# State decay and decayed scan products of the second head group moved from VectorE to ScalarE, and the chunk norm's Newton step done column by column

## The chip, the cores and the metric

The kernel runs on one core of one Trainium2 chip. Its time is device microseconds (us) of one execution of the program, and a result is the median over several executions. The core has five engines that run their own instruction queues and meet by semaphores: TensorE (PE in the profile, with PEld for its weight loads), VectorE (DVE), ScalarE (ACT), GpSimd (POOL) and SyncE (SP), which here issues all transfers.

## The reference

One layer of a hybrid generator over 1024 latent tokens of width 1024, with a prefix of 256 context tokens. A token mixer takes the normalised and modulated tokens through one input projection, whose columns feed three heads: a bidirectional state-space scan (8 heads of width 64 in two groups of four, state size 128, chunks of 128 tokens), a Fourier mix of width 256, and a pooling mix of width 256. They are joined by one output projection; then come a normalisation, and a gated feed-forward net of width 2816 with a 3x3 convolution. What the change touches is this part of the scan:

```
decay_states = jnp.exp(A_cs[..., -1:] - A_cs)
states = jnp.einsum("bclhn,bhcl,bclhp->bchpn", B, decay_states, X)
...
y_off = jnp.einsum("bclhn,bchpn,bhcl->bclhp", C, states, jnp.exp(A_cs))
return (y_diag + y_off).reshape(b, L, h, p), final_state
...
y = (y * jax.nn.silu(z.astype(jnp.float32))).reshape(bsz, L, SSD_GROUPS, SSD_WIDTH // SSD_GROUPS)
y = (y * lax.rsqrt(jnp.mean(y * y, -1, keepdims=True) + EPS)).reshape(bsz, L, SSD_WIDTH)
```

The state of each direction is multiplied at every chunk by one number per head and increased by the chunk's own contribution. The output of a chunk has a part from the state that came in, multiplied by one number per token, head and direction. The gated output is normalised over each group of 256 columns.

## The kernel before

All tensors are float32. Where TensorE needs accuracy, an operand is split into a rounded high part and a low part (`split`, lines 216 to 219: ACT writes the high part, POOL or DVE the difference), and three products are added. The program runs its stages in a row: input projection and context (0 to about 240 us), the scan, Fourier and pooling heads (to about 390), the output projection `pout` (line 1010), first normalisation (`post1`), and the feed-forward net from about 495 us to the end.

The scan has three pieces of code that matter here.

- `state_step` (lines 704 to 717), 7 steps for each of two directions: POOL weights a chunk's inputs (`xw`, line 685), TensorE makes the contribution `pst` (line 710) in PSUM, DVE multiplies the old state by `etot` (line 712, 128 tokens' worth of state rows by 512 columns: 2 groups x 4 heads x 64) and adds `pst` (line 715), and SP stores the state to DRAM (line 717). Steps 0 to 6 are spread over the projections `pf` and `pp` that feed the Fourier and the pooling head.
- `chunk_y` (line 894), once for each of 8 chunks in the order 4, 5, 6, 7, 3, 2, 1, 0: POOL starts `y` (line 900), TensorE makes `po` for either group (line 908, in PSUM, 2 directions x 4 heads x 64 columns) and `pd` (line 912), DVE multiplies both `po` tiles by the decays `ecs` into `t1` (line 914, one instruction of 512 columns per group), adds `pd` (line 918) and both directions of `t1` (line 920, twice), and multiplies by the gate (line 921). ACT takes squares with sums (line 924) and a logarithm and an exponential for a first inverse root `r` (lines 927, 928).
- `chunk_norm` (line 931) makes `r` better by one Newton step for both groups at once (`newton` with n = 2, lines 146 to 150: four instructions on a tile of 2 columns) and multiplies `y` by it (line 935). `chunk_out` (line 937) transposes `y` on TensorE (`pyt`, line 940), and ACT writes it with its weights (line 944).

`Y(i)` (line 947) writes the norm of the last chunk, the products of this one, and the output of the last one, in this order. The eight of them stand between the projections, the Fourier transforms (`four_chan` line 784, `four_dft` line 802), the pooling (`pool_sums`, `pool_res`, lines 834 to 864) and the preparation of the output weights (`wo_prep`, line 967: multiply by the gate row `g1b`, line 975, and split). The order in which the text issues instructions is not the order on the engines: a scheduler beneath the kernel places each engine's instructions by its own costs, within the dependencies and the buffers. So a change of one instruction also moves others.

PSUM holds two large tiles and four small ones (`psb`); `po`, `pd`, `pst` and `pyt` are all small ones, so TensorE's next product waits until an earlier tile has been read.

## Time and profile before

| | |
|---|---|
| time, median of 3 executions | 1211.18 us (1209.03 to 1214.26) |
| the profiled execution | 1215.51 us |
| its span, first to last instruction | 1213.7 us |
| busy: PE, PEld, DVE, ACT, POOL | 1130.9, 918.5, 991.2, 459.9, 590.2 us |
| mean granted TensorE clock | 0.981 |

The page gives busy time, idle time and the releaser of the idle time for groups of instructions. A tile's name comes without its number (`t<-po,ecs` is `t1` made from `po` and `ecs`). In rows of the timeline the first number is the start in us, the second the length in us of the row's instructions from the first's start to the last's end, and the bracket at the end is the idle time of the engine just before, with what ended it. "x4" stands for four instructions in a row. Where two instructions follow without a pause, the second starts a little before the first's end, so the time that one more instruction costs an engine is the distance of starts.

### The profile page before, as it was taken

The numbers are of one execution on the slowest core, as the hardware profiler recorded it, in microseconds if no ns is written. First come the engines' busy times: TensorE is split into PE (matmuls) and PEld (weight loads), VectorE is DVE, ScalarE is ACT, GpSimd is POOL, SyncE is SP. The second block draws the span as 40 slices with busy tenths as digits, with TensorE's granted clock in tenths as the row PEclk, the third lists the DMA queues.
The fourth block names the chain that finished last, engine by engine and source line by source line (L and its number), as shares of the span: only waits on it lengthen the run. The fifth ranks groups of instructions, "written<-read, shape, count | busy, mean of one in ns | idle before, by whom it ended". The sixth has DMA issues, their size and how long they took to land.

```text
span 1213.7 us, 15187 instructions
## 1 busy us (share of the span) xinstructions
PE 1130.9 (93%) x5328; PEld 918.5 (76%) x5328; DVE 991.2 (82%) x1407; ACT 459.9 (38%) x790; POOL 590.2 (49%) x470
## 2 busy tenths in 40 slices
PE   4899998889878998999999989999999999999986
PEld 2698887768756887788777768888888888888864
DVE  4788787688899889798999956877887787878866
ACT  2263566621444133342231333333333434333553
POOL 0010122244254024573465386767676767676756
PEclk9999999999989999999999999999999999999988
DMA  9849475557525314214545445555555565555513
GB/s 314 282 154 321 139 202 169 158 195 234 183 78 192 119 48 163 89 58 141 167 157 160 125 151 185 181 186 187 191 191 186 178 191 191 191 187 187 186 48 139
DMA packets 151875, 206.48 MB, mean 170 GB/s; under 512 B 12253, under 2 KB 89067, under 8 KB 151799
## 3 DMA queue, kind: packets, MB, share of 16 engines
q1 hardware_dynamic: 151799, 205.51, 52.4%
q8 instruction: 42, 0.69, 0.2%
q14 instruction: 34, 0.28, 0.1%
HBM read 148.76 MB, written 56.71 MB: 169 GB/s over the span
## 4 chain that ended last, share of the span: by engine, by line
PE 58%; DVE 17%; DMA 11%; POOL 4%; ACT 4%; issue 4%; SPq 1%; DVEq 0%; POOLq 0%; ACTq 0%
PE pu L1349 20%; PE pdn L1187 13%; PE pu L1521 6%; PE pout L1010 4%; DMA bc<-cs_scratch 3%; PE pl L1576 3%; PE pz L344 2%; PE p L1349 2%; PE px L445 2%; DVE cv L1234 2%; PE pu L1245 1%; DMA wa<-in_w_ada_dram 1%; DMA ctxr<-in_ctx_dram 1%; DMA wdr<-in_ffn_w_down_dram 1%; ACT EU L645 1%
## 5 line engine op out<-in xcount | busy, mean ns | idle before, releaser
L1234 DVE SCALAR_TENSOR_TENSOR cv<-pu,ffc,cv 128x945 f32<-128x945 f32 (+6 forms) x362 | 425.6, 1180 | 74.6 <-ACT cv L1212 64.9
L1187 PE MATMUL pdn<-wd,gh 128*128 128x512 f32 x576 | 182.2, 397 | 6.6 <-DVE xt L1190 6.1
L1187 PEld LDWEIGHTS pdn<-wd,gh 128*128 128x128 f32 x576 | 108.4, 189 | 33.4 <-DVE xt L1190 7.8
L1190 DVE TENSOR_TENSOR xt<-xt,pdn 128x512 f32<-128x512 f32 x128 | 87.3, 682 | 33.3 <-PE pdn L1187 28.2
L1187 PE MATMUL pdn<-wd,gl 128*128 128x512 f32 x288 | 114.1, 396 | 0.0
L219 POOL TENSOR_TENSOR wul<-wur,wuh 128x1024 fp32r<-128x1024 f32 x29 | 71.6, 2469 | 57.3 <-ACT wuh L218 42.4
L1449 POOL TENSOR_TENSOR wdr<-wdr,g2b 128x512 f32<-128x512 f32 x44 | 57.4, 1308 | 61.5 <-DMA wdr<-in_ffn_w_down_dram 61.5
L219 POOL TENSOR_TENSOR S<-wur,S 128x384 fp32r<-128x384 f32 (+2 forms) x75 | 62.1, 854 | 31.3 <-ACT S L218 30.6
L1212 ACT ACTIVATE cv<-pu,ffc 128x1024 f32<-128x1024 f32 (+3 forms) x46 | 53.5, 1165 | 43.8 <-PE pu L1349 22.1
L1475 POOL TENSOR_TENSOR cv<-cv,cv 128x512 f32<-128x512 f32 x44 | 58.6, 1351 | 22.2 <-ACT cv L1474 22.2
L1349 PE MATMUL pu<-T,S 128*128 128x512 f32 x270 | 67.1, 392 | 0.0
L644 POOL TENSOR_TENSOR bc<-bc,ncs 128x256 f32<-128x256 f32 x32 | 25.8, 810 | 79.4 <-DMA bc<-cs_scratch 68.7
L1187 PEld LDWEIGHTS pdn<-wd,gl 128*128 128x128 f32 x288 | 54.4, 189 | 12.9
L1349 PE MATMUL pu<-h2h,wuh 128*128 128x512 f32 x150 | 59.9, 400 | 3.4 <-ACT pu L1370 3.4
L219 POOL TENSOR_TENSOR gl<-cv,gh 128x512 fp32r<-128x512 f32 x44 | 57.2, 1320 | 10.9 <-ACT gh L218 10.0
L1474 ACT ACTIVATE cv<-cv 128x512 f32<-128x512 f32 x44 | 25.5, 626 | 91.8 <-DVE cv L1234 91.8
L1349 PEld LDWEIGHTS pu<-T,S 128*128 128x128 f32 x270 | 50.7, 188 | 11.6
L1349 PE MATMUL pu<-h2h,wul 128*128 128x512 f32 x150 | 59.5, 396 | 0.0
L1349 PE MATMUL pu<-h2l,wuh 128*128 128x512 f32 x150 | 59.2, 395 | 0.0
L206 POOL TENSOR_TENSOR h2l<-h2t,h2h 128x512 fp32r<-128x512 f32 x14 | 20.6, 1478 | 77.6 <-DVE h2h L205 77.6
L219 POOL TENSOR_TENSOR wd<-wdr,wd 128x512 fp32r<-128x512 f32 x42 | 53.7, 1301 | 4.4 <-ACT wd L218 4.2
L1521 PE MATMUL pu<-h2h,wuh 128*128 128x512 f32 x176 | 55.6, 397 | 0.0
(407 smaller groups left out, 2923.5 us busy)
## 6 DMA issues: line engine op xcount, KB each, us to landing
xt<-x_scratch SPq DMA_DIRECT2D x144, 256.0 KB
x_scratch<-xt SPq DMA_DIRECT2D x144, 256.0 KB
wur<-in_ffn_w_up_dram SPq DMA_DIRECT2D x44, 512.0 KB
wad<-in_w_ada_dram SPq DMA_DIRECT2D x32, 512.0 KB
wdr<-in_ffn_w_down_dram SPq DMA_DIRECT2D x44, 256.0 KB
wa<-in_w_ada_dram SPq DMA_DIRECT2D x32, 256.0 KB
bc<-cs_scratch SPq DMA_DIRECT2D x32, 256.0 KB
xr<-in_x_dram SPq DMA_DIRECT2D x8, 512.0 KB
```

Of the source, the lines that this page charges most:

```text
L219: return (eng or G).tensor_tensor(lo, raw, hi.bitcast(F32), op=ALU.subtract)
L644: G.tensor_tensor(bc[:, 1], bc[:, 1], ncs[:, ch, b : b + 2].unsqueeze(2).broadcast_to([P, 2, P]), op=ALU.add)
L1010: TE.matmul(pt[:, nb * 512 : nb * 512 + 512], u, v[:, nb * 512 : nb * 512 + 512], start=first and i == 0, stop=last and i == 2)
L1187: TE.matmul(pt, u_, wd[nb][:, v_, :], start=i == 0, stop=i == n - 1)
L1190: V.tensor_tensor(xt, xt, pt, op=ALU.add)
L1212: tap[0] = S.activation(acc[:, a * 64 : b * 64], pt[:, a * 64 : b * 64], AF.Identity, bias=ffc[:, 396 + ct : 397 + ct], scale=factor(0, 0))
L1234: last = V.scalar_tensor_tensor(dst, pv[:, r0 + dy : r1 + dy, c0 + dx : c1 + dx], factor(dy, dx), dst, op0=ALU.mult, op1=ALU.add)
L1349: TE.matmul(dst, a[k][u], b[k][w], start=start and k == 0 and j == 0, stop=k == n - 1 and j == 2, skip_group_check=True)
L1449: G.tensor_tensor(raw, raw, g2b[:, s], op=ALU.mult)
L1475: G.tensor_tensor(acc[:, s], acc[:, s], acc_v[:, s], op=ALU.mult)
L1521: TE.matmul(pt[:, q * 512 : q * 512 + 512], a[:, k, :], b[q][:, k, :], start=k == 0 and j == 0, stop=k == KD - 1 and j == 2)
L1576: TE.matmul(accs[t][nb], u_, wd[nb][:, v_, :], start=t < NHALF and m == 0 and i == 0, stop=m == NG - 1 and i == 2, skip_group_check=t >= N ...
```

## The change

Three edits. (1) In `state_step`, DVE multiplies only the first group of the state (256 columns); ACT multiplies the second in four instructions of 64 columns, one per head, with the decay as a scale that is one number per partition. (2) In `chunk_y`, DVE makes the product of the first group only; ACT makes the second group's in eight instructions of 64 columns. (3) `chunk_norm` runs `newton` with n = 1 for each of the two groups (lines 141 to 144: three instructions on one column, in which `r` and `v` are also the per-partition scalars) and multiplies each half of `y` by its own column.

```diff
         dst, src = qt(stag[d](), f"st{d}_{n + 1}", [P, 2, 256]), state[d]
-        V.tensor_tensor(dst[:].rearrange("p g (h q) -> p g h q", q=64),
-                                      src[:].rearrange("p g (h q) -> p g h q", q=64),
-                                      dv(etot, ch, d).unsqueeze(3).broadcast_to([P, 2, 4, 64]), op=ALU.mult)
+        V.tensor_tensor(dst[:, 0].rearrange("p (h q) -> p h q", q=64), src[:, 0].rearrange("p (h q) -> p h q", q=64),
+                        dv(etot, ch, d)[:, 0].unsqueeze(2).broadcast_to([P, 4, 64]), op=ALU.mult)
+        for h in range(4):
+            S.activation(dst[:, 1, h * 64 : h * 64 + 64], src[:, 1, h * 64 : h * 64 + 64], AF.Identity,
+                         scale=etot[:, ch, 8 + 4 * d + h : 9 + 4 * d + h])
         V.tensor_tensor(dst, dst, pt[:].rearrange("p (g n) -> p g n", g=2), op=ALU.add)
...
-        for g in range(2):
-            V.tensor_tensor(t1[:, g].rearrange("p d (h q) -> p (d h) q", q=64),
-                            pos[g][:].rearrange("p (a q) -> p a q", q=64),
-                            ecs[:, ch, g * 8 : g * 8 + 8].unsqueeze(2).broadcast_to([P, 8, 64]), op=ALU.mult)
+        V.tensor_tensor(t1[:, 0].rearrange("p d (h q) -> p (d h) q", q=64), pos[0][:].rearrange("p (a q) -> p a q", q=64),
+                        ecs[:, ch, 0:8].unsqueeze(2).broadcast_to([P, 8, 64]), op=ALU.mult)
+        for a in range(8):
+            S.activation(t1[:, 1, a // 4, (a % 4) * 64 : (a % 4) * 64 + 64], pos[1][:, a * 64 : a * 64 + 64], AF.Identity,
+                         scale=ecs[:, ch, 8 + a : 9 + a])
...
         V.tensor_scalar(v, ssq, 1.0 / 256.0, EPS, op0=ALU.mult, op1=ALU.add)
-        r = newton(r, v, 2, f"ssn{ch}")
-        V.tensor_tensor(yv, yv, r.unsqueeze(2).broadcast_to([P, 2, 256]), op=ALU.mult)
+        for g in range(2):
+            q = newton(r[:, g : g + 1], v[:, g : g + 1], 1, f"ssn{ch}{g}")
+            V.tensor_scalar(yv[:, g], yv[:, g], q, None, op0=ALU.mult)
```

The added lines shift what follows: line 715 before is 717 now, 918 is 921, 920 is 923, 921 is 924, 933 is 936, 935 is 939, 940 is 944, 971 is 975 and 975 is 979. The order on the engines changes between about 243 and 400 us of the old span; behind that it is the same but for a few transfers. Three places are spoken of below.

TensorE, where the projection `pp` of the second half of the pooling columns meets the first chunk's transposes (`pyt`, of chunk 4) and the Fourier head's products (`pft`, `pex`). Before, and then now:

```order
L445 MATMUL pp_2891<-hl_193,wp_h 128x512
L445 MATMUL pp_2891<-hl_194,wp_h 128x512
L940 MATMUL pyt_2837<-ident,y_2762 128x128 x4
L784 MATMUL pft_2870<-PQW,f_2469 128x128 x4
L784 MATMUL pft_2876<-PQW,f_2469 128x128 x4
L787 MATMUL pex_2882<-fex_2478,PQW 128x2
L908 MATMUL po_2928<-S_2794,cT_1341 128x256 x2
```

```order
L445 MATMUL pp_2966<-hh_191,wp_h 128x512
L445 MATMUL pp_2966<-hh_192,wp_h 128x512
L944 MATMUL pyt_2912<-ident,y_2818 128x128 x2
L786 MATMUL pft_2945<-PQW,f_2477 128x128 x4
L786 MATMUL pft_2951<-PQW,f_2477 128x128
L944 MATMUL pyt_2912<-ident,y_2818 128x128 x2
L786 MATMUL pft_2951<-PQW,f_2477 128x128 x3
L789 MATMUL pex_2957<-fex_2486,PQW 128x2
L445 MATMUL pp_2966<-hl_193,wp_h 128x512
```

Between the last `pd` of chunk 5 and the transposes of chunk 4 stood 23 pairs of `pp` matmuls; now 10 stand there, and 13 follow.

VectorE, at the first two chunks (`y_2762` and `y_2818` are chunk 4's `y`, `y_2807` and `y_2875` chunk 5's; `wor` is an output weight that waits for `g1b`). Before, directly behind the multiplication of `wor`, and then now:

```order
L914 TENSOR_TENSOR t_4_2764<-po_2765,ecs 128x512
L914 TENSOR_TENSOR t_4_2764<-po_2768,ecs 128x512
L918 TENSOR_TENSOR y_2762<-y_2762,pd_2771 128x512
L920 TENSOR_TENSOR y_2762<-y_2762,t_4_2764 128x512 x2
L918 TENSOR_TENSOR y_2807<-y_2807,pd_2816 128x512
L921 TENSOR_TENSOR y_2762<-y_2762,z_2655 128x512
```

```order
L915 TENSOR_TENSOR t_4_2820<-po_2821,ecs 128x512
L979 TENSOR_TENSOR wor_3176<-wor_3176,g1b 128x1024
L921 TENSOR_TENSOR y_2818<-y_2818,pd_2827 128x512
L923 TENSOR_TENSOR y_2818<-y_2818,t_4_2820 128x512 x2
L924 TENSOR_TENSOR y_2818<-y_2818,z_2695 128x512
```

The weight's multiplication went from ahead of the first product to behind it.

SyncE, at the last states (`st_6`, `st_7`) and the load of `g1b`. Before, and then now:

```order
L717 DMA s_scratch<-st_6_2716 128x512
L971 DMA g1b<-ada_scratch 128x1024
L717 DMA s_scratch<-st_7_2737 128x512
L717 DMA s_scratch<-st_7_2746 128x512
L886 DMA S_2794<-s_scratch 128x1024
```

```order
L719 DMA s_scratch<-st_6_2760 128x512
L719 DMA s_scratch<-st_7_2785 128x512
L975 DMA g1b<-ada_scratch 128x1024
L719 DMA s_scratch<-st_7_2798 128x512
L888 DMA S_2857<-s_scratch 128x1024
```

The load of `g1b` went behind the store of the first of the last two states.

## The prediction, made before the changed kernel was run

> **What bounds the kernel now.** I read the busy time by stretch first. Each row gives the stretch, its length, then busy us (and instructions) of PE, PEld, DVE, ACT and POOL, the granted clock, and DMA.
>
> ```profile
> 240.00:290.00 50.00, 44.90 (x202) 36.76 (x201) 42.19 (x82) 8.58 (x17) 23.63 (x23) 0.97 0.63 209
> 290.00:390.00 100.00, 82.76 (x415) 67.92 (x415) 93.11 (x145) 39.42 (x101) 40.94 (x20) 0.93 0.50 158
> 390.00:440.00 50.00, 50.00 (x218) 39.94 (x217) 37.76 (x97) 10.26 (x23) 0.00 (x0) 1.00 0.31 110
> 440.00:495.00 55.00, 50.48 (x244) 40.87 (x243) 52.13 (x113) 22.75 (x44) 27.05 (x16) 0.97 0.34 111
> 495.00:1160.00 665.00, 654.00 (x2808) 528.56 (x2807) 552.89 (x544) 233.78 (x367) 435.24 (x351) 0.99 0.52 167
> ```
>
> The reader is to see that the change sits in the first two rows, and that they differ. From 240 to 290 us PE is busy for 44.9 of 50, so work taken from DVE there lies mostly behind matmuls. From 290 to 390 DVE is busy for 93.1 of 100 and PE for only 82.8: here DVE sets the pace and PE loses 17.2 us. From 390 on PE runs without a gap, and what follows moves as a whole when PE gets there earlier. So the change is worth what it takes from PE's 17.2 us, plus a little ahead of them. The largest of PE's waits, from its timeline:
>
> ```profile
> 291.82 1.13 PE L908 MATMUL po<-S,cT 128*128 128x256 f32 x4 [0.40 <-DVE t L914]
> ...
> 307.75 0.93 PE L940 MATMUL pyt<-ident,y 128*128 128x128 f32 x4 [2.34 <-DVE s L863]
> ...
> 343.68 0.73 PE L1010 MATMUL pout<-woh,yh 128*128 128x512 f32 x2 [1.87 <-ACT yh L218]
> ...
> 360.11 1.98 PE L871 MATMUL ppool<-pT,PQW 128*128 128x512 f32 x4 [2.55 <-DVE pT L864]
> ...
> 386.65 1.08 PE L940 MATMUL pyt<-ident,y 128*128 128x128 f32 x4 [3.03 <-DVE y L935]
> ```
>
> Four of the five end with DVE: each time PE has caught up with DVE's queue. The last, at 386.65, is chunk 1's transpose; behind it PE is never short again. So DVE's progress up to the end of chunk 1's norm counts.
>
> **The change part by part.** First the scan products (edit 2) and the price of one DVE instruction:
>
> ```profile
> L914 DVE TENSOR_TENSOR t<-po,ecs 128x512 f32<-128x512 f32 x16 | 10.5, 681 | 0.8 <-PE po L908 0.7
> ...
> 296.00 1.28 DVE L914 TENSOR_TENSOR t<-po,ecs 128x512 f32<-128x512 f32 x2
> ...
> 284.60 1.28 DVE L712 TENSOR_TENSOR st<-st,etot 128x512 f32<-128x512 f32 x2
> ...
> L811 DVE TENSOR_TENSOR f<-py,yo 128x256 f32<-128x256 f32 x2 | 0.8, 412 | 0.0
> ```
>
> Of 16 products of 0.68 us, 8 leave DVE. Two in a row take 1.28, so one costs the queue 1.28 - 0.68 = 0.60 us. Seven of the eight lie ahead of the wait at 386.65 (chunk 0's comes behind it): 7 x 0.60 = **-4.2 us** on DVE's path. PE's wait of 0.40 at 291.82 is for a small PSUM tile that DVE frees late, behind its load of `g1b`; now the first group's tile is freed ahead of that and the second's by ACT: **-0.4**.
>
> What ACT takes over has no row of its size. The nearest are these; the last two show how long PE's own `pd` takes and when the next stage of PE began:
>
> ```profile
> L944 ACT ACTIVATE yT<-pyt,col 128x128 f32<-128x128 f32 x32 | 9.3, 367 | 22.2 <-PE pyt L940 22.2
> ...
> 308.72 1.15 ACT L944 ACTIVATE yT<-pyt,col 128x128 f32<-128x128 f32 x4 [5.23 <-PE pyt L940]
> ...
> L158 ACT ACTIVATE pn_s<-pn_v 128x1 f32<-128x1 f32 x16 | 3.2, 203 | 26.4 <-DVE pn_v L156 26.4
> ...
> 313.59 1.89 PE L912 MATMUL pd<-xt,M 128*128 128x64 f32 x16
> ...
> 319.05 1.89 PE L908 MATMUL po<-S,cT 128*128 128x256 f32 x8
> ```
>
> With 128 columns one more costs (1.15 - 0.37) / 3 = 0.26 us; a single column lasts 0.20. For 64 columns I take 0.23 (bounds 0.15 and 0.26). Eight are 8 x 0.23 + 0.13 = 2.0 us, starting when `po` is complete. In that time PE is at `pd` for 1.9 us, and DVE cannot add `pd` (0.68) before; the additions of `t1` come after that, at about 2.5 us. So the eight lie behind `pd`, if ACT is free. It is busy for 39.4 of 100 us and gets 64 x 0.23 = 14.7 more. I take 0; if another ACT instruction of 1 us is ahead each time, the chunk is late by 0.5, and over seven chunks that is at most +3.5.
>
> **The state decay (edit 1).** Half of 14 multiplications leaves: 14 x (0.68 - 0.41) = 3.8 us of DVE, between 243 and 287 us. What hides it is `pf` and `pp` on PE. Only PE's idle time can give something, and its largest piece is this one, with the two transfers that matter at the end of the stretch and who waits for the second:
>
> ```profile
> 265.13 1.08 PE L738 MATMUL pPQ<-cf 128*128 128x64 f32 x8 [3.40 <-DMA cf<-in_fnet_w_dram]
> ...
> 261.25 0.32 SPq L717 DMA_DIRECT2D s_scratch<-st  x1
> ...
> 285.07 0.44 SPq L971 DMA_DIRECT2D g1b<-ada_scratch  x1
> ...
> 286.50 1.03 SPq L717 DMA_DIRECT2D s_scratch<-st  x2
> ...
> 289.94 1.22 DVE L975 TENSOR_TENSOR wor<-wor,g1b 128x1024 f32<-128x1024 f32 x1 [2.87 <-DMA g1b<-ada_scratch]
> ```
>
> The second part of `cf` was queued behind the store of a state at 261.25, and now stands ahead of both stores; it can be issued about 0.7 us earlier: **-0.7** (0 to -1.5). Against it stands the wait that this edit adds: the addition of `pst` now waits for ACT's four pieces. Where two steps follow each other, as at 284.60, DVE needed 4 x 0.60 = 2.4 us; now the second direction's pieces end at 8 x 0.23 + 0.13 = 2.0 and its addition takes 0.68, so 2.7, that is 0.3 late. Behind these additions are queued the stores, and behind the first store now also `g1b`: it was issued at 285.07 and would go at about 286.0 to 286.8. It took 289.94 - 285.07 = 4.9 us to arrive, so DVE's multiplication of `wor`, and behind it in DVE's queue chunk 4's additions, start at 291 to 291.7 in place of 289.94. But one product stands ahead of it now (0.60) and one is gone (0.60), so chunk 4's last addition is at most 0.6 late, or as it was. I take 0 and keep +1.5. If the cover of PE's matmuls were gone in steps 0 to 5, each step would cost some 0.3, in all +2.
>
> **The norm (edit 3).** The old chain where nothing disturbs it, two Newton chains on one column interleaved (from `post1`), and a multiplication of 1024 columns by scalars:
>
> ```profile
> 360.16 0.16 DVE L146 TENSOR_TENSOR ssn_t<-sr 128x2 f32<-128x2 f32 x1
> ...
> 361.56 1.22 DVE L975 TENSOR_TENSOR wor<-wor,g1b 128x1024 f32<-128x1024 f32 x1
> ...
> 466.73 0.27 DVE L141 TENSOR_SCALAR ln_t<-ln_r,ln_v 128x1 f32<-128x1 f32 x1
> ...
> 467.54 0.20 DVE L175 TENSOR_SCALAR ln_nmr<-ln_mv,ln_q 128x1 f32<-128x1 f32 x1
> ...
> 473.22 0.80 DVE L320 TENSOR_SCALAR xn<-xa,ln_mv,ln_q 128x1024 f32<-128x1024 f32 x1
> ...
> 473.94 1.28 DVE L170 BATCH_NORM_STATS2 pn_st<-xa 128x6 f32<-128x512 f32 x2
> ```
>
> Old: from 360.16 to 361.56, 1.40 us for four small instructions and the multiplication. New: six small ones took 467.54 - 466.73 = 0.81. The multiplication of 1024 columns costs 473.94 - 473.22 = 0.72; a [128,1] instruction about 0.13; so 256 columns cost 0.13 + 0.59 / 4 = 0.28, and two 0.56. New: 1.37. I take 0, with 0.2 either way for seven chunks: -1.5 to +1.5.
>
> The small instructions also meet POOL:
>
> ```profile
> 303.35 2.39 POOL L975 TENSOR_TENSOR wor<-wor,g1b 128x1024 f32<-128x1024 f32 x1 [9.96 <-DVE s L843]
> ...
> 303.37 2.38 DVE L150 TENSOR_TENSOR ssn_q<-sr,ssn_t 128x2 f32<-128x2 f32 x1
> ...
> 446.89 5.08 POOL L206 TENSOR_TENSOR h2l<-h2t,h2h 128x512 fp32r<-128x512 f32 x3 [1.50 <-DVE h2h L205]
> ...
> 447.25 0.27 DVE L141 TENSOR_SCALAR pn_t<-pn_r,pn_v 128x1 f32<-128x1 f32 x1
> ...
> L914 DVE TENSOR_TENSOR t<-po,ecs x16: 672/680/693, 291.1 to 387.0; 128x512 f32<-128x512 f32 x16
> ...
> L920 DVE TENSOR_TENSOR y<-y,t x16: 676/692/2661, 293.0 to 390.1; 128x512 f32<-128x512 f32 x16
> ```
>
> An old Newton instruction of two columns was held for all of POOL's 2.39 us; the one-column form ran in its usual 0.27 under POOL. So the new chain is not held. But the next instruction, the multiplication of `y`, reads SBUF like those that are held, so the stall goes to it: 0, bounds -2 to 0. The last two rows speak against edit 2: the product from PSUM never lasts longer than 0.69, while the addition from SBUF to SBUF goes up to 2.66. The Trainium skill has a rule for this ("SBUF — State Buffer", section "SBUF: two separate sides"): VectorE and GpSimd share a port pair as an exclusive lock, which a VectorE instruction needs if it has two SBUF inputs, and one from PSUM does not. The trace agrees with it in these rows. By it the edit takes away the very work that DVE could do while POOL holds the port; what that makes of the time is the second rival.
>
> **The sum.** -4.2 - 0.4 - 0.7 = **-5.3 us**, so 1215.51 - 5.3 = 1210.2 for an execution like the profiled one. That one was 4.3 us above the median of the runs shown; against the median it is 1211.18 - 5.3 = **1205.9 us**, 0.44% less. The unknown terms (ACT late +3.5, `g1b` +1.5, norm -1.5 to +1.5, stall -2, `cf` -0.8 to +0.7) seldom all fall on one side: about 1202 to 1210.
>
> **The rivals.** First, *more than DVE's share*: the queues' new order also takes away waits. Chunk 1's transposes stand later in PE's order, so the wait of 3.03 at 386.65 can go; half of it and of the 1.87 at 343.68 would be -2.5, with the stall's -2 that is 1205.9 - 4.5 = 1201.4. For it: these waits are PE's order against DVE's. Against: DVE still has 89 us of work for these 100.
>
> Second, *less, because POOL holds DVE anyway*. POOL is busy 40.9 of the 100 us. If that share of the products ran while POOL held the port, 0.41 x 4.2 = 1.7 us of them cost nothing before, and their leaving saves nothing; if the weights' preparation on POOL and ACT (the waits at 343.68) then sets the pace for another 2, only -5.3 + 3.7 = -1.6 is left: 1209.6. For it: L920's 2.66. Against: DVE's queue had other work from PSUM, too.
>
> Third, *slower: chunk 4's transposes stand too early*. These rows give PE's pace before them and DVE's last instruction for them:
>
> ```profile
> 294.49 0.71 PE L445 MATMUL pp<-hh,wp_h 128*128 128x512 f32 x2
> ...
> 304.79 0.62 PE L445 MATMUL pp<-hl,wp_h 128*128 128x512 f32 x2
> ...
> 306.93 0.68 DVE L935 TENSOR_TENSOR y<-y,ssn_q 128x512 f32<-128x512 f32 x1
> ```
>
> Before, 23 pairs, one per (304.79 - 294.49) / 22 = 0.468 us, covered chunk 4's norm, which ended at 307.6. Now only 10 do: PE is there at 294.1 + 4.7 = 298.8. With a wait w, then 13 pairs (6.1) and the work from 307.75 to 319.05 (11.3), PE comes to chunk 7's `po` at 316.2 + w, against 319.05: it decides at w = 2.85, that is with `y` ready at 301.6. I expect about 301: chunk 4's norm has moved ahead of the pooling sums. If the late `g1b` and ACT's queue keep it at 307.6, w is 8.8 and 5.9 us are lost. DVE's saving then lies idle: 1211.2 + 5.9 = 1217.1.
>
> **How the numbers follow.** A change under 0.5% (6 us) is about what a measurement of this kernel cannot tell from none. Chances: forecast 0.45, about 1202 to 1210 with the edge of 0.5% at 1205.1, so 0.17 of it faster and 0.28 the same; first rival 0.22, all but 0.01 faster; second 0.17, the same; third 0.16, 0.12 of it slower and the rest, with a smaller w, the same. That makes faster 0.38, same 0.50, slower 0.12. The range leaves out a tenth on either side, so it cuts into both outer cases: 1199.5 to 1215. The forecast's own is 1202 to 1210.
>
> **What would show it.** DVE's busy time from 290 to 390 down by 4 to 5 us; ACT up by 14 to 15 there, its pieces starting 0.2 to 0.25 us apart; the span down by as much as PE's idle time in this stretch; the one-column Newton instructions never above 0.3 us, and the halves of line 939 held in their place; the wait at chunk 4's transposes under 2.9 us; the feed-forward net, from 495 on, of the same length. I am wrong if DVE is 5 us lighter and PE's idle time is the same, or if ACT's pieces end behind the addition of `pd`.

## The result, and the profile after

The changed kernel took 1204.0 us (median of five executions; 1202.95 to 1205.81) against 1211.18 us (also of five; 1209.03 to 1214.26). The ratio is 0.9939 (95% interval 0.9919 to 0.9960), so it is faster by 0.61%, some 7 us. That is a little more than the 0.5% which the prediction took as the least that a measurement tells from none; 1205.9 us had been forecast. The profiled execution took 1203.6 us, with a span of 1201.8 us and a mean granted clock of 0.983.

Three of the same stretches of the changed kernel, busy us (and instructions) of PE, PEld, DVE, ACT and POOL, then clock and DMA:

```profile
240.00:290.00 50.00, 46.84 (x221) 38.92 (x220) 40.51 (x86) 25.91 (x92) 24.18 (x23) 0.97 0.73 235
290.00:390.00 100.00, 84.43 (x424) 67.91 (x423) 90.64 (x176) 53.23 (x158) 37.56 (x19) 0.95 0.51 171
...
495.00:1160.00 665.00, 650.29 (x2782) 525.49 (x2781) 556.02 (x548) 233.24 (x367) 438.89 (x356) 0.99 0.52 168
```

From 290 to 390 us DVE is lighter by 2.5 us only (4 to 5 had been forecast) and ACT heavier by 13.8, and PE still loses 15.6 of 100 us (17.2 before). Read by fixed windows, little has happened. The stretches have moved against the work in them, though, so I cut the two traces at matmuls that stand behind the same work in both. These are the starts on TensorE of the second `pinit`, chunk 4's first `po`, chunk 7's first `po`, the second `ppool`, and the first `h` of the normalised output. Before, from the timeline (chunk 7's `po` at 319.05 and the second `ppool` at 360.11 stand in the prediction), and then after:

```profile
244.42 0.38 PE L698 MATMUL pinit<-xwc,btc 128*128 128x256 f32 x1
...
286.88 0.38 PE L908 MATMUL po<-S,cT 128*128 128x256 f32 x1
...
417.59 0.27 PE L189 MATMUL h<-ident,xn 128*128 128x128 f32 x1
```

```profile
240.15 0.38 PE L698 MATMUL pinit<-xwc,btc 128*128 128x256 f32 x1
...
280.61 0.38 PE L910 MATMUL po<-S,cT 128*128 128x256 f32 x1
...
308.18 0.38 PE L910 MATMUL po<-S,cT 128*128 128x256 f32 x1
...
346.87 3.78 PE L873 MATMUL ppool<-pT,PQW 128*128 128x512 f32 x4 [6.60 <-DVE pT L866]
...
366.77 0.44 PE L944 MATMUL pyt<-ident,y 128*128 128x128 f32 x2 [2.24 <-DVE y L939]
...
380.78 0.63 PE L944 MATMUL pyt<-ident,y 128*128 128x128 f32 x4 [2.14 <-DVE y L939]
...
406.79 0.27 PE L189 MATMUL h<-ident,xn 128*128 128x128 f32 x1
```

The 11.9 us between the two spans divide like this. Ahead of the second `pinit`, where order and work are the same, 4.3 us: chance of these two executions. To chunk 4's `po`: 42.46 and 40.46, **-2.0**. From there to chunk 7's `po`: 32.17 and 27.57, **-4.6**. From there to the second `ppool`: 41.06 and 38.69, **-2.4**. From there to the first `h`: 57.48 and 59.92, **+2.4**. Behind it -1.1. The changed part gives -6.5 us, which agrees with the medians.

At the start of the last of these stretches TensorE has stood for 6.60 us ahead of the second pooling matmul (2.55 before), and within it TensorE waits for `y` at the transposes of chunks 2 and 0, at 366.77 and 380.78. What TensorE gained ahead of the pooling it partly lost again there.

### The profile page after: what moved, and what is told of

Read it like the earlier page. It is cut to its first block, busy times and chain, and to the rows that moved or that the text cites. A ratio compares the mean times of both kernels' runs of the same rounds, so it can differ in the third digit from the quotient of the medians.

```text
span 1201.8 us, 15357 instructions
## 1 busy us (share of the span) xinstructions
PE 1128.6 (94%) x5328; PEld 916.5 (76%) x5328; DVE 979.1 (81%) x1423; ACT 486.7 (40%) x910; POOL 588.0 (49%) x470
## 4 chain that ended last, share of the span: by engine, by line
PE 64%; DVE 15%; DMA 8%; POOL 5%; ACT 4%; issue 3%; SPq 0%; DVEq 0%; POOLq 0%; ACTq 0%
PE pu L1353 21%; PE pdn L1191 14%; PE pu L1525 6%; PE pout L1014 4%; PE pz L344 4%; PE px L445 3%; PE pl L1580 3%; PE p L1353 2%; DMA bc<-cs_scratch 2%; PE pu L1249 2%; DVE cv L1238 2%; PE pf L445 1%; DMA wa<-in_w_ada_dram 1%; DMA x_scratch<-xt 1%; PE pst L710 1%
## 5 line engine op out<-in xcount | busy, mean ns | idle before, releaser
L219 POOL TENSOR_TENSOR wul<-wur,wuh 128x1024 fp32r<-128x1024 f32 x29 | 71.4, 2464 | 58.9 <-ACT wuh L218 44.1
L219 POOL TENSOR_TENSOR S<-wur,S 128x384 fp32r<-128x384 f32 (+2 forms) x75 | 62.2, 855 | 29.5 <-ACT S L218 29.5
L219 POOL TENSOR_TENSOR gl<-cv,gh 128x512 fp32r<-128x512 f32 x44 | 57.7, 1331 | 12.6 <-ACT gh L218 12.4
L1353 PE MATMUL pu<-h2h,wuh 128*128 128x512 f32 x150 | 59.9, 400 | 3.1 <-ACT pu L1374 3.1
```

The lines of the kernel that those rows point to most:

```text
L219: return (eng or G).tensor_tensor(lo, raw, hi.bitcast(F32), op=ALU.subtract)
L1353: TE.matmul(dst, a[k][u], b[k][w], start=start and k == 0 and j == 0, stop=k == n - 1 and j == 2, skip_group_check=True)
```

## The experiments

Each run below has its change against the kernel before (95% interval), and one trace. The table gives both; the three stretches, in us, are those from the second `pinit` to chunk 4's `po` (A), from there to the second `ppool` (B), and from there to the first `h` (C). "Stalls" is the time by which DVE's instructions from the second `pinit` to the first `h` took longer than the shortest of the same operation and shape there, summed over the timeline's rows.

| kernel | time against before | A | B | C | stalls |
|---|---|---|---|---|---|
| before | | 42.5 | 73.2 | 57.5 | 32.0 |
| before again | +0.04% (-0.09 to +0.17) | 43.3 | 71.5 | 58.6 | 30.0 |
| state only | -0.19% (-0.32 to -0.06) | 39.1 | 73.1 | 59.9 | 29.5 |
| products only | -0.41% (-0.60 to -0.22) | 44.5 | 66.3 | 58.1 | 25.3 |
| norm only | -0.54% (-0.73 to -0.34) | 44.2 | 70.5 | 55.8 | 25.4 |
| state and products | -0.80% (-1.03 to -0.56) | 39.2 | 68.8 | 58.2 | 25.1 |
| state and norm | -0.75% (-1.00 to -0.51) | 39.4 | 72.9 | 55.8 | 23.8 |
| products and norm | -0.29% (-0.44 to -0.14) | 44.7 | 66.7 | 60.7 | 29.0 |
| all three (the change) | -0.61% (-0.81 to -0.40) | 40.5 | 66.3 | 59.9 | 25.4 |
| Newton by column | -0.37% (-0.56 to -0.18) | 38.6 | 69.7 | 55.8 | 24.5 |
| halves only | -0.06% (-0.22 to +0.10) | 44.6 | 70.6 | 58.9 | 30.6 |
| change, later transposes | -0.84% (-1.07 to -0.61) | 39.4 | 67.9 | 58.3 | 25.7 |
| change, less on POOL | -1.01% (-1.29 to -0.74) | 39.7 | 67.8 | 55.0 | 22.1 |
| change, early products only | -0.59% (-0.74 to -0.44) | 37.4 | 66.6 | 57.7 | 22.9 |

A stretch of one trace is good to some 1 to 2 us: the two traces of the kernel before differ by 0.8, 1.7 and 1.1. So is the column of stalls, which also moves by 1 or 2 us with the way in which rows of several instructions are counted. A trace is of one execution, which can lie off its kernel's median, most of all for Newton by column (1203.07 us against 1209.24), the early products (1200.62 against 1205.5) and state and norm (1205.75 against 1202.36).

**The kernel before, again** (no edit):

> The kernel before, once more, for its spread. Expected: 0 within 0.2%. By the two profiles the stretch ahead of the change (start to the second pinit, 244.42 us against 240.15) differed by 4.3 us although work and order there are the same; if that is chance, this profile lies anywhere from 240 to 245 there, with the stretch from the second pinit to the first transpose of the normalised output (173.17 us) within 1 us, and the wait for cf stays about 3.4. If the cf wait itself changes by more than 1 us, part of what edit 1 seems to give is chance too.

The time is the same. Its second `pinit` stood at 241.10 us, so the 4.3 us ahead of the change are chance. The wait for `cf` was 1.52 us, not 3.40: part of it comes and goes by chance. Stretch A was no shorter for it, as TensorE had already lost 2 us ahead of that wait: from 247 to 255 us its granted clock was 0.81.

**One edit alone.** The state decay:

```diff
-        V.tensor_tensor(dst[:].rearrange("p g (h q) -> p g h q", q=64),
...
+        V.tensor_tensor(dst[:, 0].rearrange("p (h q) -> p h q", q=64), src[:, 0].rearrange("p (h q) -> p h q", q=64),
...
+        for h in range(4):
+            S.activation(dst[:, 1, h * 64 : h * 64 + 64], src[:, 1, h * 64 : h * 64 + 64], AF.Identity,
```

> Only the state decay is changed (edit 1); TensorE's order stays that of the kernel before. Theory A (the prediction): the load of cf goes 0.7 us earlier, nothing else: -0.7 us, the wait at the first pPQ falls from 3.40 to about 2.7. Theory B (the transfers' order is worth more than the prediction gave it): in the changed kernel's trace that wait is gone altogether and the stretch from the second pinit to chunk 4's first po is 40.46 us against 42.46 before, so -2.0 us, with pPQ not waiting. Theory C (chance: the two profiled executions differ ahead of the change as well): 0, and cf waits as before.

Measured -0.19%, about -2.3 us, and stretch A is 3.3 to 4.1 us shorter than in the two traces of before. Theory B holds for the place: the wait at the first `pPQ` went down to 0.65 us. Some of it was lost again in C. The queue of transfers of the kernel before:

```profile
255.29 0.45 SPq L884 DMA_DIRECT2D M<-m_scratch  x1
260.08 0.32 SPq L717 DMA_DIRECT2D s_scratch<-st  x1
260.68 0.33 SPq L732 DMA_DIRECT2D cf<-in_k_c_dram  x1
...
261.62 0.42 SPq L733 DMA_DIRECT2D cf<-in_fnet_w_dram  x1
```

and in that of the changed kernel:

```profile
255.96 0.33 SPq L734 DMA_DIRECT2D cf<-in_k_c_dram  x1
256.34 0.43 SPq L735 DMA_DIRECT2D cf<-in_fnet_w_dram  x1
256.86 1.18 SPq L719 DMA_DIRECT2D s_scratch<-st  x2
```

The queue stood from 255.7 to 260.08 for the first of the two stores, which waits for DVE's addition, and both parts of `cf` were behind it. Now they are ahead of both stores, and in the changed kernel's trace the second part was issued 3.5 us ahead of the `pPQ` at 259.87 that needs it. The new place alone does not explain the gain, though. In the state-only kernel the second part was issued at 257.95 us, 17.1 us behind the second `pinit`, and before the change 17.2 behind it: the queue now stood until 257.57 for another instruction of DVE. What differs is what came after. `pPQ` began 2.1 us behind the issue, not 3.5, and the matmuls that follow ran faster. `pPQ` and one of the pairs of `pf` matmuls behind it in the state-only kernel, and the same pair before (`pPQ` with its wait of 3.40 stands in the prediction):

```profile
260.02 1.08 PE L740 MATMUL pPQ<-cf 128*128 128x64 f32 x8 [0.65 <-DVE gt L630]
...
262.37 0.63 PE L445 MATMUL pf<-hh,wf_h 128*128 128x512 f32 x2
```

```profile
267.89 1.05 PE L445 MATMUL pf<-hh,wf_h 128*128 128x512 f32 x2
```

Twelve `pf` matmuls follow `pPQ`. They took 4.4 us before, at a granted clock of 0.61 (266.0 to 270.4 us), and 2.9 us in the state-only kernel, at 1.00 (260.9 to 263.7). So about 1.5 us of the gain are matmuls that ran slowly behind the long wait and no longer do. Why `cf` comes faster behind its issue is not shown.

The scan products:

```diff
-        for g in range(2):
-            V.tensor_tensor(t1[:, g].rearrange("p d (h q) -> p (d h) q", q=64),
...
+        V.tensor_tensor(t1[:, 0].rearrange("p d (h q) -> p (d h) q", q=64), pos[0][:].rearrange("p (a q) -> p a q", q=64),
...
+        for a in range(8):
+            S.activation(t1[:, 1, a // 4, (a % 4) * 64 : (a % 4) * 64 + 64], pos[1][:, a * 64 : a * 64 + 64], AF.Identity,
```

> Only the scan products are changed (edit 2). Theory A (the prediction): DVE's queue is lighter by 0.60 us at each of seven chunks, so TensorE's lead grows from chunk to chunk up to the last chunk's transposes: -4.6 us. Theory B (order): what counts is that chunk 4's transposes now stand behind 12 or 13 pp pairs and not 23, and find y ready: then the gain is there before chunk 7's po (the stretch from chunk 4's first po to chunk 7's first po, 32.17 us before and 27.57 in the changed kernel, falls to 28 to 29) and nothing is added behind it: -3 to -4. The two are told apart by the stretches, not by the sum.

Measured -0.41%, about -5.0 us: the size of theory A (-4.6). The place is that of neither theory alone. Stretch B is 5 to 7 us shorter, half of it ahead of chunk 7's `po` and half behind; C is as before.

The norm:

```diff
-        r = newton(r, v, 2, f"ssn{ch}")
-        V.tensor_tensor(yv, yv, r.unsqueeze(2).broadcast_to([P, 2, 256]), op=ALU.mult)
+        for g in range(2):
+            q = newton(r[:, g : g + 1], v[:, g : g + 1], 1, f"ssn{ch}{g}")
+            V.tensor_scalar(yv[:, g], yv[:, g], q, None, op0=ALU.mult)
```

> Only the norm is changed (edit 3); DVE keeps all 16 products. Theory A (the prediction): 0 (-1.5 to +1.5), since six small instructions and two halves cost what four and one whole did. Theory B (order): the old Newton chain of chunk 4 took from 299.99 to 306.93 us because an instruction of about 1.2 us was put into each gap between its dependent steps; the new one took from 290.03 to 293.43 in the changed kernel. With that alone the transposes move ahead of some pairs, the wait of 2.34 us at 307.75 and the slow matmuls behind it (3.33 against 1.95 us) go: -2.5 to -4, all of it before chunk 7's po.

Measured -0.54%, about -6.5 us, with all 16 products still on DVE. Theory A (0) is wrong. Theory B (-2.5 to -4) is too small and has the wrong place: the wait at chunk 4's transposes was still 1.92 us, and the time from chunk 4's to chunk 7's `po` was 31.89, as before. The gain lies behind that, up to the second `ppool` and in C. In this one trace B and C together are 3.9 to 4.5 us shorter than in the two traces of before; the rest of the 6.5 us does not show in the stretches.

**What in the norm edit pays.** The first half alone keeps one multiplication of 512 columns:

```diff
-        r = newton(r, v, 2, f"ssn{ch}")
-        V.tensor_tensor(yv, yv, r.unsqueeze(2).broadcast_to([P, 2, 256]), op=ALU.mult)
+        q = sm.tile([P, 2], F32, tag="rq2", name=f"ssn{ch}_q")
+        for g in range(2):
+            t, rg = sm.tile([P, 1], F32, tag="rt1", name=f"ssn{ch}{g}_t"), r[:, g : g + 1]
+            V.tensor_scalar(t, rg, rg, v[:, g : g + 1], op0=ALU.mult, op1=ALU.mult)
+            V.tensor_scalar(t, t, -0.5, 1.5, op0=ALU.mult, op1=ALU.add)
+            V.tensor_scalar(q[:, g : g + 1], t, rg, None, op0=ALU.mult)
+        V.tensor_tensor(yv, yv, q.unsqueeze(2).broadcast_to([P, 2, 256]), op=ALU.mult)
```

> Half of edit 3: the Newton step runs column by column (three one-column instructions each), but y is still multiplied by both columns in one instruction of 512 columns. TensorE's order is nearly that of the kernel before (43 pp matmuls ahead of chunk 4's transposes, 46 before, 35 in the norm-only kernel). Edit 3 alone measured -0.54%, about -6.5 us, with DVE's stalls (time above the usual length of the same instruction) down from 32.0 to 25.4 us. Theory H (the one-column instructions are not held while POOL works, so some 5 us of stalls go): -3 to -6 us, stalls at 25 to 27 us. Theory O (the gain is TensorE's new order): -1 us or less, since the order hardly moves. Theory V (the gain is in the two halves): -1 us or less.

The second half alone keeps the old Newton step:

```diff
-        r = newton(r, v, 2, f"ssn{ch}")
-        V.tensor_tensor(yv, yv, r.unsqueeze(2).broadcast_to([P, 2, 256]), op=ALU.mult)
+        q = newton(r, v, 2, f"ssn{ch}")
+        for g in range(2):
+            V.tensor_scalar(yv[:, g], yv[:, g], q[:, g : g + 1], None, op0=ALU.mult)
```

> The other half of edit 3: the old Newton step on two columns (four instructions), then two multiplications of 256 columns by a scalar per partition. TensorE's order is nearly as before (44 pp matmuls ahead of chunk 4's transposes). Theory H (the old small instructions are what POOL holds): 0 to -1 us, stalls at 29 to 32 us. Theory O: -1 us or less. Theory V (the first half's transposes start before the second half is done, and an instruction of 256 columns by a scalar is short): -3 to -6 us.

The one-column Newton step gave -0.37%, the halves -0.06%, with TensorE's order nearly that of before in both. So theory H: it is the form of the small instructions. (That stretch A is short in the trace of the first, 38.6 us, is chance: its `cf` was issued 14.5 us behind the second `pinit`, and `pPQ` waited 0.16 us.) Chunk 1's norm shows the cause, the one behind the wait of 3.03 us at 386.65 in the kernel before. There, POOL and DVE:

```profile
380.30 1.04 POOL L900 TENSOR_TENSOR y<-xt,skip 128x512 f32<-128x512 f32 x1 [7.58 <-DVE ssn_t L147]
381.30 2.36 POOL L975 TENSOR_TENSOR wor<-wor,g1b 128x1024 f32<-128x1024 f32 x1
383.62 2.34 POOL L219 TENSOR_TENSOR yl<-yT,yh 128x1024 fp32r<-128x1024 f32 x1
...
380.31 1.05 DVE L148 TENSOR_SCALAR ssn_t<-ssn_t 128x2 f32<-128x2 f32 x1
381.40 2.27 DVE L150 TENSOR_TENSOR ssn_q<-sr,ssn_t 128x2 f32<-128x2 f32 x1
383.71 2.80 DVE L935 TENSOR_TENSOR y<-y,ssn_q 128x512 f32<-128x512 f32 x1
```

and in the norm-only kernel, with TensorE's transposes behind it:

```profile
376.06 1.04 POOL L900 TENSOR_TENSOR y<-xt,skip 128x512 f32<-128x512 f32 x1 [7.64 <-PE pyt L941]
377.06 2.40 POOL L976 TENSOR_TENSOR wor<-wor,g1b 128x1024 f32<-128x1024 f32 x1
...
376.42 0.27 DVE L142 TENSOR_SCALAR ssn_t<-ssn_t 128x1 f32<-128x1 f32 x2
376.61 0.33 DVE L144 TENSOR_SCALAR ssn_q<-ssn_t,sr 128x1 f32<-128x1 f32 x2
376.86 2.76 DVE L936 TENSOR_SCALAR y<-y,ssn_q 128x256 f32<-128x256 f32 x2
...
379.67 0.44 PE L941 MATMUL pyt<-ident,y 128*128 128x128 f32 x2 [0.44 <-DVE y L936]
```

Before, three instructions in a row were held, each until one of POOL's ended: from 380.31 to 386.51, 6.2 us for a chain that needs about 1. In the new form the small ones pass and only the multiplication is held: from 376.42 to 379.62, 3.2 us. The wait of 3.03 became 0.44.

**Two edits of three.** Without the state decay, without the products, without the norm (each is the change's diff less that part):

> The changed kernel without edit 1. TensorE's order is exactly that of the changed kernel. Edit 1 alone measured -0.19%, about -2.3 us. If the edits' gains simply added, this kernel would be 2.3 us slower than the changed one, -0.42% against before. They do not add: products -5.0, norm -6.5 and state -2.3 make -13.8, and the changed kernel has -7.4. Theory E (edit 1 brings TensorE to the scan earlier, where DVE then is the bound, so its gain is given back at the next waits): this kernel is at -0.5 to -0.65%, the same as the changed one within 1.5 us. Theory S (sum): -0.42%.

> The changed kernel without edit 2 (state decay and norm). TensorE's order is that of the norm-only kernel. By the prediction's terms it should be -0.7 and 0, so about -0.1%. By the single runs' sum it would be -2.3 - 6.5 = -8.8 us, -0.73%. If what is to be had ends at some 7 us (the wait for pT at the second pooling matmul, 6.96 us in the norm-only kernel, and POOL's chain take what DVE saves), it is -0.55 to -0.65%, no different from the norm alone, and then edit 2 adds nothing to the other two.

> The changed kernel without edit 3 (state decay and products): by the prediction's terms this is where its gain sits, -5.3 us (-0.44%), and the norm adds nothing. By the runs so far (products alone -0.41%, state alone -0.19%, norm alone -0.54%, state and norm -0.75%, all three -0.61%) edit 1 is worth about as much in company as alone. Theory A (the prediction's parts): -0.45%, the same as all three. Theory N (the norm is what brings most, and products and norm overlap): -0.4 to -0.6%, with DVE's stalls from the second pinit to the first h at 25 to 30 us and the stretch from the second pooling matmul's wait to the first h at 58 us, as in the products-only run.

The state decay adds in any company: -0.19% alone, -0.39% on the products, -0.21% on the norm, -0.32% on both, in the mean -0.28% or 3.4 us, and it lies in stretch A (37.4 to 40.5 us with it; 42.5 to 44.7 without it, and by chance once 38.6). The run without it is nearer to theory S than to E. Products and norm do not add: each is worth 0.4 to 0.6% alone or on the state decay, and whichever comes second on top of the other gains nothing (+0.12 to +0.25%, within the intervals). State and norm, without the edit that the prediction lived on, add as single runs (-0.73% by their sum, -0.75% measured), and are as fast as the full change; products without norm are too (-0.80%, more than either theory had, with stalls and stretch C as theory N said). The column of stalls says the same: 29.5 to 32 us with neither, 23.8 to 25.4 with either, 25.4 and 29.0 with both.

**Where it is given back.** Stretch C is 55.8 us with the norm alone, 58.1 with the products alone and 59.9 to 60.7 with both. There, in the changed kernel, POOL and DVE:

```profile
354.49 2.36 POOL L219 TENSOR_TENSOR wol<-wor,woh 128x1024 fp32r<-128x1024 f32 x1 [0.72 <-DVE yl L219]
356.81 1.49 POOL L902 TENSOR_TENSOR y<-xt,skip 128x512 f32<-128x512 f32 x1
358.26 2.84 POOL L979 TENSOR_TENSOR wor<-wor,g1b 128x1024 f32<-128x1024 f32 x1
...
355.36 3.49 DVE L923 TENSOR_TENSOR y<-y,t 128x512 f32<-128x512 f32 x2
358.88 2.77 DVE L924 TENSOR_TENSOR y<-y,z 128x512 f32<-128x512 f32 x1
```

and in the norm-only kernel, where DVE makes both products of chunk 2:

```profile
365.59 2.83 POOL L976 TENSOR_TENSOR wor<-wor,g1b 128x1024 f32<-128x1024 f32 x1
...
363.02 3.15 DVE L920 TENSOR_TENSOR y<-y,t 128x512 f32<-128x512 f32 x2
366.21 2.76 DVE L921 TENSOR_TENSOR y<-y,z 128x512 f32<-128x512 f32 x1
...
354.41 3.78 PE L871 MATMUL ppool<-pT,PQW 128*128 128x512 f32 x4 [6.96 <-DVE pT L864]
```

In both, DVE gets through chunk 2 when POOL ends: 14.8 us behind the start of the second `ppool` with the change (361.65 - 346.87), 14.6 us in the norm-only kernel (368.97 - 354.41). In the products-only kernel it is 14.6 too, and before it was 13.2, each time 0.5 to 0.6 us behind the end of POOL's multiplication. The product that DVE no longer makes had cost nothing there that shows. In TensorE's order, though, the transposes stand earlier now: those of chunk 2 behind 63 `pout` matmuls, in the norm-only kernel behind 70, and chunk 0's behind 90, there behind 111.

Waits are not the whole difference. Stretch C of the kernel before, of products only, norm only and the change, in the columns of the prediction's first view:

```profile
360.11:417.59 57.48, 52.19 (x245) 41.81 (x246) 50.26 (x93) 20.76 (x50) 13.55 (x7) 0.97 0.49 168
351.40:409.50 58.10, 54.52 (x245) 43.08 (x246) 44.33 (x87) 25.63 (x74) 13.52 (x7) 0.93 0.47 165
354.40:410.16 55.76, 53.54 (x245) 41.53 (x246) 47.39 (x104) 20.76 (x50) 13.70 (x7) 0.96 0.50 171
346.87:406.79 59.92, 54.30 (x245) 42.72 (x246) 47.65 (x102) 25.47 (x74) 13.69 (x7) 0.93 0.47 158
```

TensorE has the same 245 matmuls in each. With products only it is idle for 3.6 us of C and before for 5.3, so the lighter DVE did save it 1.7 us; but the matmuls themselves took 2.3 us more, at a granted clock of 0.93 in place of 0.97. From norm only to the change, the 4.2 us are 3.4 of waiting and 0.8 of slower matmuls. Some of the slow ones are the second `ppool` itself: four matmuls in 1.98 us behind a wait of 2.55 before, in 3.78 us behind waits of 6.96 and 6.60 in the last two. No run sets the clock by itself, so how much of C's length is due to it stays open. Three kernels try the waits.

The transposes of chunks 2 and 1 written later:

```diff
             if i > 0:
-                chunk_out(*lastc[0])
+                if hold:
+                    outs[i] = lastc[0]
+                else:
+                    chunk_out(*lastc[0])
...
+    def out_of(i):
+        return lambda: chunk_out(*outs[i])
...
-        3: [Y(6)],
-        4: [Y(7)],
+        3: [Y(6, True)],
+        4: [Y(7, True)],
+        6: [out_of(6), out_of(7)],
```

> All three edits, and the transposes of chunks 2 and 1 are issued later in the text, so that on TensorE they stand behind 72 pout matmuls (the changed kernel: 63, the norm-only kernel: 70), and chunk 0's behind 108 (90, 111). In the changed kernel TensorE waits 2.24, 0.83 and 2.14 us at these three; the norm-only kernel waits 0.44 there, although y of chunk 2 is ready in both 20 us after the second pooling matmul began. Theory P (the transposes stand too early there): the stretch from the second pooling matmul's start to the first h falls from 59.9 to 56 to 57 us, the time by 3 to 4 us, to -0.85 to -0.95%. Theory D (DVE's queue sets the end of this stretch, wherever TensorE's order puts the transposes): the waits move to other places, and the time stays within 1 us of the changed kernel's, -0.55 to -0.65%.

Stretch C fell by 1.6 us and not by 3 to 4. The waits at the transposes went, and TensorE stood 3.28 us at another place, for DVE's sum of the first output tile (line 1035):

```profile
295.95 0.66 PE L944 MATMUL pyt<-ident,y 128*128 128x128 f32 x2 [2.77 <-DVE ssn_q L144]
...
382.87 0.74 PE L1022 MATMUL pout<-woh,yh 128*128 128x512 f32 x2 [3.28 <-DVE xa L1035]
```

The trace is more theory D than P: the waits moved. The time of -0.84% is about what P had forecast, but its interval overlaps with that of the changed kernel, so the times do not decide between the two.

Two of POOL's multiplications left out:

```diff
-        (G if i % 2 else V).tensor_tensor(raw, raw, g1b[0], op=ALU.mult)
+        if i % 2 == 0 or i < 4:
+            (G if i % 2 else V).tensor_tensor(raw, raw, g1b[0], op=ALU.mult)
```

> All three edits, with two of POOL's multiplications of an output weight by the gate row left out (those weights stay unscaled, so this part of the output is not computed; the later two of the four on POOL). In the changed kernel these two start at 358.26 (2.84 us) and 367.86 (2.35 us); during the first DVE's multiplication of chunk 2's y by the gate lasts 2.77 us, not 0.69, and during the second one half of chunk 1's norm lasts 1.10, not 0.35. Theory H (POOL holds DVE and so takes back what edit 2 gives): DVE's stalls fall by 3 us or more, the waits at the transposes of chunks 2 and 1 (2.24 and 0.83) go below 1 us together, the time falls by 2 to 4 us to -0.8 to -0.95%. Theory Q (the weights' chain itself sets the pace: the split of a weight follows its multiplication): the waits go from the transposes to pout, and the time falls by less than 1 us. Where neither chain nor hold counts: 0.

Stretch C fell by 4.9 us and the stalls by 3.3; the time went to -1.01%. That is at least theory H's size. But waits of 0.97 and 1.80 us at transposes remained (at 366.97 and 376.17), 2.1 of the 4.9 us are faster matmuls (52.22 us busy, at a clock of 0.96), and the weights also came earlier, so the hold and the weights' chain are not fully parted by it.

The products on ACT only ahead of the pooling:

```diff
+        late = ch in (2, 1, 0)
+        for g in range(2 if late else 1):
+            V.tensor_tensor(t1[:, g].rearrange("p d (h q) -> p (d h) q", q=64),
...
+        for a in range(0 if late else 8):
+            S.activation(t1[:, 1, a // 4, (a % 4) * 64 : (a % 4) * 64 + 64], pos[1][:, a * 64 : a * 64 + 64], AF.Identity,
```

> All three edits, but the second group's products are by ACT only for chunks 4, 5, 6, 7 and 3; for chunks 2, 1 and 0 DVE makes both again. TensorE's order behind the pooling follows: chunk 1's transposes stand behind 81 pout matmuls (63 in the changed kernel), chunk 0's behind 104 (90), chunk 2's behind 64 (63). The stretch from chunk 4's first po to the second pooling matmul took 71.5 to 73.2 us where DVE makes all products and 66.3 to 68.8 where ACT makes half; the one behind it, to the first h, took 55.8 with the norm edit alone and 59.9 to 60.7 with norm and products. Theory L (products on ACT pay ahead of the pooling and cost behind it): the first stays at 66 to 69, the second falls to 56 to 57, the time is 2 to 4 us below the changed kernel's, -0.8 to -0.95% against before. Theory M (behind the pooling POOL's hold sets the end, whoever makes the products, and the placement of the transposes moves waits only): the second stays at 58 to 60 and the time at -0.6 to -0.7%.

The time is that of the changed kernel: theory M. (Its trace is of the fastest of six executions, so its stretches flatter it.) No kernel that computes the whole is shown to beat the changed one; the intervals of those with -0.75 to -0.84% overlap with its own.

## Why the prediction was right, and where it was not

The time, its sign and its size were right (forecast -5.3 us, measured about -7.2). The sum's terms were not, and the size is right by luck, as point 4 shows.

1. **"-4.2 us on DVE's path" for the products.** Right in size for the edit alone (-5.0 measured against -4.6 with the PSUM tile's 0.4). Wrong in how it comes about: it was to grow by 0.60 a chunk up to the last transposes, which is 3.0 us in stretch B (five chunks) and 1.2 in C (two). Stretch B gained 5 to 7 us, and C's length nothing. On top of the norm edit it is worth nothing that these runs can show. The step that failed is the one that took DVE's instruction count as its pace: DVE's stalls, which the count leaves out, fell by another 5 to 7 us, and at chunk 2, behind the pooling, DVE's pace is POOL's. The second rival had said so and had its rows, L914 at 0.69 and L920 at 2.66; it was right for chunk 2 and wrong for B. In C as a whole TensorE did wait 1.7 us less than before, and slower matmuls took that back.

2. **"-0.7 (0 to -1.5)" for `cf`.** Mis-sized: -3.4 us in the mean of four comparisons. The term priced an earlier issue. In the state-only kernel the issue was not earlier; `cf` came faster behind it, and the term had nothing for the matmuls behind the wait, which took 4.4 us before and 2.9 without the long wait.

3. **"I take 0" for the norm.** Wrong: alone -6.5 us. The working held that the stall would pass from the small instructions to the multiplication of `y` (-2 to 0). At chunk 1 that is what the multiplication did; but the two small ones ahead of it had been held as well, each for another of POOL's instructions, and that part (3 us there) went. The hint stood in the prediction's own rows: 2.38 us for an instruction on two columns.

4. **What made the sum right** is that 2 and 3 were too small by some 9 us, and that products and norm do not add (-0.29% against -0.41 - 0.54 = -0.95%, which is 8 us; on the state decay -0.61% against -0.19 - 0.61 - 0.56 = -1.36%, 9 us). Either takes some 5 to 7 us of stalls from DVE, and both together no more. The edits were costed one by one on the same queue and added; that they would share one gain was not considered. Two errors of opposite sign met: that is luck.

5. **ACT's lateness at 0 (bound +3.5).** Right in effect: DVE never waited for these pieces. Its price of 2.0 us for eight was 1.74. At six chunks they ended before the addition of `pd` did; at chunks 5 and 1 they waited for the tile `t1` of the chunk before, and ended 1.0 and 1.4 us behind that addition, while DVE had other work. The prediction had named this as a sign of being wrong, and it cost nothing. The group by its tile (shortest, median, longest in ns):

```profile
L918 ACT ACTIVATE t<-po,ecs x64: 295/324/368, 282.5 to 372.8; 128x64 f32<-128x64 f32 x64
```

Eight pieces of the state decay and the first eight of the products, from ACT's timeline:

```profile
276.35 2.02 ACT L715 ACTIVATE st<-st,etot 128x64 f32<-128x64 f32 x8 [3.53 <-DVE st L717]
282.53 1.74 ACT L918 ACTIVATE t<-po,ecs 128x64 f32<-128x64 f32 x8 [4.17 <-PE po L910]
```

6. **The third rival, chunk 4's transposes too early.** Its condition came about in three of the five traces with state decay and products: waits of 3.39, 2.77 and 2.59 us at these transposes, about its break-even of 2.85. It goes with the late `g1b`, as it had said: in these three DVE's multiplication by `g1b` waited 3.0 to 3.5 us for it, in the other two 0.3 and 0.5. Those kernels did not end slower: from chunk 7's `po` to the second `ppool` the three took 36.3 us, the changed kernel 38.7, so a part of the loss was made up further on. The two rows, of the changed kernel and of the one with later transposes:

```profile
282.69 1.23 DVE L979 TENSOR_TENSOR wor<-wor,g1b 128x1024 f32<-128x1024 f32 x1 [0.32 <-DMA g1b<-ada_scratch]
```

```profile
286.26 1.23 DVE L987 TENSOR_TENSOR wor<-wor,g1b 128x1024 f32<-128x1024 f32 x1 [3.15 <-DMA g1b<-ada_scratch]
```

7. **Two readings of the rows.** "Behind it PE is never short again" does not hold: by the prediction's own fourth row TensorE was busy for 50.5 of the 55 us from 440 on. Nothing in the sum rests on that. The waits that it called the largest leave out one of 1.84 us at chunk 7's transposes and three of 1.3 to 1.4.

What stays open: why products and norm together lose 4 to 5 us in C against the norm alone, and how much of it is the clock. The transposes' place gave 1.6 of it back, less work on POOL 4.9, DVE making the late products itself 2.2 in a trace that flatters; none of the three gave a time that is surely below the change's.

## What to carry to other kernels

Where two engines share something, price an instruction by how long it is held in that stretch and not by its usual length: a chain of small instructions can be held once for each of the other engine's, and changing their form can be worth more than moving large ones away. Edits that relieve the same queue must be costed together, since the second finds the slack already gone; run them alone and in pairs before crediting one. And price a wait of TensorE together with the matmuls behind it: here twelve of them took 4.4 us behind a long wait and 2.9 behind a short one.

## What the runs showed of the hardware that was not expected

One-column instructions by a scalar were never held by POOL in these traces, some of them in the middle of POOL's work (at 376.42 and 376.61 us of the norm-only kernel), while an instruction on two columns was held just as well as one on 512. After and then before, all of the scan's norms (count, then shortest, median and longest in ns):

```profile
L141 DVE TENSOR_SCALAR ssn_t<-sr,sv x16: 255/266/274, 290.0 to 379.7; 128x1 f32<-128x1 f32 x16
L144 DVE TENSOR_SCALAR ssn_q<-ssn_t,sr x16: 198/204/214, 291.1 to 380.2; 128x1 f32<-128x1 f32 x16
L939 DVE TENSOR_SCALAR y<-y,ssn_q x16: 338/348/2449, 291.8 to 380.5; 128x256 f32<-128x256 f32 x16
```

```profile
L148 DVE TENSOR_SCALAR ssn_t<-ssn_t x8: 152/162/1051, 301.9 to 395.7; 128x2 f32<-128x2 f32 x8
L150 DVE TENSOR_TENSOR ssn_q<-sr,ssn_t x8: 107/386/2383, 303.4 to 396.0; 128x2 f32<-128x2 f32 x8
```

A multiplication by a per-partition scalar, which has one tile and that scalar as inputs, was held too when it had 256 columns (up to 2.45 us), and so was an instruction on two columns by constants (L148, up to 1.05). The Trainium skill ("SBUF — State Buffer", section "SBUF: two separate sides") names two kinds of VectorE instruction that need the port pair shared with GpSimd: those with two SBUF inputs, and those in a 2-port mode. These rows agree if the scalar instructions on two and more columns are of the second kind and those on one column are of neither; no run here shows an instruction's mode.
